# The second MLP product over both token halves at once, each of its seven products again split in seven

## The chip, the cores and the metric

The kernel runs on one core of one Trainium2 chip. TensorE (PE in the profile) multiplies matrices into PSUM; VectorE (DVE), ScalarE (ACT) and GpSimd (POOL) work element by element; SyncE (SP) issues the transfers between HBM and on-chip memory (SBUF). Each engine has its own instruction queue, works through it in order, and waits on semaphores of the others. The metric is the device time of one execution in microseconds; the time before is the median of three runs. All data are float32.

## The reference

A layer of an encoder with 2048 tokens of width 1024: a mixer with two groups of attention heads, an output projection, and an MLP of width 4096. Only the MLP matters for the change:

```python
h = rmsnorm(x, g_norm2[l]) * (1.0 + sc2) + sh2
x = x + gt2 * (jnp.square(jax.nn.relu(h @ w1[l])) @ w2[l])
```

`h` is 2048 x 1024, `w1` 1024 x 4096, `w2` 4096 x 1024. Below, `h @ w1` is the first product, the product with `w2` the second, and the squared ReLU between them gives the hidden values.

## The kernel before

**Precision.** TensorE multiplies in a rounded float32. To keep float32 accuracy, each operand is split in a high part (ACT copies it into the rounded type) and a low part (DVE subtracts the high part from the source): `split`, lines 123 to 125. A product of two tiles is then three matmuls, high x high, high x low and low x high (`mm3`). A split is thus one ACT and one DVE instruction for each tile of 128 x 512, and both inputs of the DVE instruction lie in SBUF.

**Seven products.** Both MLP products use a scheme in which a product of 2 x 2 blocks is formed from seven block products instead of eight (Winograd's form of Strassen's). The seven have numbers 1 to 7. Their operands are blocks or sums and differences of blocks, and the four result blocks are running sums of the products.

**Stages.** The tokens form two halves of 1024 (`mb` 1, then 0), each of two blocks of 512 (`TB`). For each half there are 7 x 16 steps of the first product (`First(mb, j, i)`; column group `j` of 16, product `i` of seven), then 7 x 16 steps of the second (`Second(mb, i, j)`). A step is 12 matmuls. `First` takes the activations from `hops[i, k]`, split tiles that stay in SBUF for a whole half, and splits its weight tile (`opw` in the profile). After each column group DVE and ACT form the hidden blocks (`hidden`: two ACT activations), and DVE the differences that the second product needs; SP stores all seven to HBM (`scr_hid`).

`Second` before: for product `i`, 16 row groups `j`, each step with a hidden tile and a weight tile of 128 x 512, both loaded from HBM in pairs (`hw`) and both split (`oph`, `opv`): two splits for 12 matmuls into four PSUM banks. At the end of each product four sums out of PSUM are made.

**Weight sums.** The first product's weight sums are four POOL sums in each column group (`sums`, tiles `ts` and `w`), with both inputs in SBUF. Those of `w2` are made while the first product of half 1 runs: `second_sums`, 64 DVE sums of 128 x 512 (`w2s`), stored to `scr_s`.

**Norm and blocks of half 0.** The norms of half 0 (`norm2`) and its activation blocks (`right_blocks(0, k, temp)`, scaled, split and subtracted on DVE and ACT) are spread over the second product of half 1.

**What sets the order.** The main loop at the end walks over the list `steps`. Before step `n` runs, it prepares (splits) the operands of later steps as long as at most 8 operand tiles are ready or in use (`opp`, 8 buffers). Then it runs the jobs that `at(n, job)` has entered for that step, then the step's matmuls and what follows them; `later.add(t, job)` runs a job t steps later. The order in which the program emits instructions is the order of each engine's queue. TensorE and SP keep exactly this order, and the other engines too work in the order of emission. Raw tiles come from `ring` (3 buffers) and `spare` (1), accumulators and kept blocks from `accp` (12), temporary ones from `tp` (7).

Of the kernel before, what the change touches and what calls it, by code (L numbers as in the profile page):

```python
# [18 lines left out]
P = 128  # L19
# [60 lines left out]
def encoder_kernel(ctx, tc, xT, c, g1, g2, w_in, w_rest, gqk, bias, w_o, w1, w2, w_ada, b_ada, out):  # L80
# [1202 lines left out]
    PRODUCTS = (1, 6, 5, 7, 2, 3, 4)  # L1283
    scr_hid = scratch("scr_hid", [P, 2, TB], 2, 8, NP // 2)
    scr_s = scratch("scr_s", [P, 2, TB], 7, NP // 2)

    pm = ctx.enter_context(ExitStack())
    if True:
# [42 lines left out]
        def norm2(tb, step):  # L1331
# [26 lines left out]
            for k in range(KT):  # L1358
                at(step + k, lambda k=k: load(k))
                at(step + k + 4, lambda k=k: add(k))  # L1360
            at(step + KT + 4, lambda: later.add(2, second))
# [54 lines left out]
        class Step:  # L1416
            tiles = frees = 1

            def prepare(self):
                pass  # L1420
# [4 lines left out]
        class First(Step):  # L1425
# [4 lines left out]
            def __init__(self, mb, j, i):  # L1430
                self.mb, self.j, self.i, self.nm = mb, j, i, f"{mb}_{j}_{i}"
                if mb and j == 0 and i in PRODUCTS[:2]:
                    self.tiles = self.frees = 0
# [35 lines left out]
            def run(self):  # L1469
                d, i, nm = First.pair[self.mb, self.j], self.i, self.nm  # L1470
                home = {2: 1, 4: 7}.get(i, i)
# [8 lines left out]
                if i == 1:  # L1480
                    d["u"] = kept(f"u{nm}")
                    act.copy(d["u"], ps)
                if i == 6:
                    column_sum(dve, d["u"], ps, d["u"], ALU.add)
                if i == 5:
                    d["v"] = column_sum(dve, kept(f"v{nm}"), ps, d["u"], ALU.add)
                if i == 7:
                    d["c22"] = self.hidden(column_sum(dve, kept(f"x{nm}"), ps, d["v"], ALU.add), 3)
# [6 lines left out]
                if i == 3:  # L1495
                    c12 = self.hidden(column_sum(dve, d["v"], ps, d["v"], ALU.add))

                    def rest():
                        t1 = column_sum(dve, kept(f"a{nm}"), c12, d["c11"], ALU.subtract)
                        self.keep(5, t1)  # L1500
                        d["t2"] = column_sum(dve, kept(f"b{nm}"), d["c22"], t1, ALU.subtract)
                        self.keep(6, d["t2"])
                        self.keep(7, column_sum(dve, c12, d["c22"], c12, ALU.subtract))

                    later.add(2, rest)
                if i == 4:
                    c21 = self.hidden(column_sum(dve, d["u"], ps, d["u"], ALU.add), 2)
# [17 lines left out]
        def second_sums(j, step):  # L1525
# [3 lines left out]
            def load():  # L1529
                t.append(raw_pair([P, 2, 2, TB], F32, f"w2s_{j}"))  # L1530
                for s in range(2):
                    sp.dma_start(t[0][:, s].rearrange("p r n -> p (r n)"), w2[2 * j + s])

            def out(i, dst, a, b, op):
                tile = {nm: t[0][:, s, r, :] for nm, s, r in (("11", 0, 0), ("21", 0, 1), ("12", 1, 0), ("22", 1, 1))}
                column_sum(dve, tile[dst], tile[a], tile[b], op)
                sp.dma_start(scr_s[i - 1 if i < 7 else 0, j // 2][:, j % 2, :], tile[dst])

            at(step - (6 if j else 0), load)
            sums = ((5, "22", "21", "22", ALU.add), (7, "21", "11", "21", ALU.subtract))  # L1540
            sums += ((6, "11", "22", "11", ALU.subtract), (3, "12", "12", "11", ALU.subtract))
            for n, x in enumerate(sums):
                at(step + n + (0 if j else 4), lambda x=x: out(*x))

        class Second(Step):


            tiles = frees = 2
            banks, raws, whole = {}, {}, {}

            def __init__(self, mb, i, j):
                self.mb, self.i, self.j, self.nm = mb, i, j, f"{mb}_{i}_{j}"

            def load(self):
                mb, i, j = self.mb, self.i, self.j
                t = raw_pair([P, 2, 2, TB], F32, f"hw{self.nm}")
                h, w = t[:, 0], t[:, 1]
                sp.dma_start(h, scr_hid[mb, i, j // 2])
                if i in (1, 2, 4):
                    r, s = {1: (0, 0), 2: (0, 1), 4: (1, 1)}[i]  # L1560
                    for q in range(2):
                        sp.dma_start(w[:, q, :], w2[2 * (j + q) + s][:, r * TB : (r + 1) * TB])
                else:
                    sp.dma_start(w, scr_s[i - 1 if i < 7 else 0, j // 2])
                Second.raws[mb, i, j // 2] = h, w

            def prepare(self):
                mb, i, j = self.mb, self.i, self.j
                h, w = Second.raws[mb, i, j // 2]
                self.h = operand(h[:, j % 2, :], f"h{self.nm}")  # L1570
                self.w = operand(w[:, j % 2, :], f"v{self.nm}")

            def run(self):
                mb, i, j = self.mb, self.i, self.j
                if j == 0:
                    Second.banks[i] = [bank(f"{self.nm}_{n}") for n in range(HK)]
                if i not in (1, 6, 5):
                    if j == NP // 2 - 1:
                        self.load_base()
                    if NP // 2 + 2 < j <= NP // 2 + 2 + HK:  # L1580
                        self.base(j - NP // 2 - 3)
                for n in range(HK):
                    ns = slice(n * P, (n + 1) * P)
                    mm3(
                        Second.banks[i][n], self.w[:, 0, ns], self.w[:, 1, ns], self.h[:, 0, :], self.h[:, 1, :],
                        j == 0, j == NP - 1,
                    )
                if j == NP - 1:
                    for n in range(HK):
                        self.out(n, Second.banks[i][n])  # L1590

            def load_base(self):
                i, d = self.i, Second.whole
                for n in range(HK):
                    d["x", n] = temp(f"x{self.nm}_{n}")
                    sp.dma_start(d["x", n], scr_x[2 * self.mb + (i in (2, 4)), n + HK * (i in (7, 4))])

            def base(self, n):

                i, d = self.i, Second.whole  # L1600
                nn = n + HK * (i in (7, 4))
                x, u = d["x", n], d[{7: "v", 2: "s", 3: "v", 4: "u"}[i], n]
                dve.scalar_tensor_tensor(x, u, mod[:, 5 * KT + nn : 5 * KT + nn + 1], x, op0=ALU.mult, op1=ALU.add)

            def out(self, n, ps):
                i, d = self.i, Second.whole
                tb = 2 * self.mb + (i in (2, 4))
                if i == 1:
                    d["s", n] = kept(f"s{self.nm}_{n}")
                    act.copy(d["s", n], ps)  # L1610
                    return
                if i == 6:
                    d["u", n] = column_sum(dve, kept(f"u{self.nm}_{n}"), ps, d["s", n], ALU.add)
                    return
                if i == 5:
                    d["v", n] = column_sum(dve, kept(f"v{self.nm}_{n}"), ps, d["u", n], ALU.add)
                    return
                if i == 7:
                    column_sum(dve, d["u", n], ps, d["u", n], ALU.add)
# [178 lines left out]
```

## Time and profile before

| | |
|---|---|
| median of three runs | 2596.46 us (2596.16 to 2598.76) |
| span of the profiled execution | 2595.2 us |
| stage of the first product, half 1 | 1365.7 to 1671.6 us |
| second product, half 1 | 1671.6 to 1977.5 us |
| first product, half 0 | 1977.5 to 2284.0 us |
| second product, half 0, and the end | 2284.0 to 2595.2 us |

In the profile, times are microseconds from the start of the span unless marked ns. A row of a group of instructions gives the engine, the operation, output <- inputs by the program's tile names, the shape, the count, then busy time in all and mean ns of one, then idle time just before and what ended it. A row of a tile gives minimum, median and maximum ns. A row of the view in order of time gives start, duration, engine and operation. Durations of neighbouring instructions of an engine can overlap by some 0.1 us, so the price of one in a dense row is taken from start to start. Every instruction of the kernel stands at line 42 (L42), since a helper there issues it; the tile names tell them apart.

### The profile page before, as it was taken

To read this page: it belongs to the slowest core of one execution; us is meant where nothing else is said; L and a number is where in the kernel's file an instruction comes from. 1 tells how busy PE (TensorE), PEld (TensorE's weight loads), DVE (VectorE), ACT (ScalarE), POOL (GpSimd) and SP (SyncE) were. 2 spreads that over 40 slices of the span, in tenths; PEclk is the share of its full clock that TensorE was granted. 3 is DMA by queue.
4 is the path that set the end of the run, shared out by engine and by line. 5 is a ranking of instruction groups with operands and counts; after the bars stand their busy time and mean duration, and the time that the engine had idled before them with its cause. 6 is when DMAs were issued, how large, how long until landed. Compare 5 with 4: busy or idle time off the path is not lost.

```text
span 2595.2 us, 39377 instructions
## 1 busy us (share of the span) xinstructions
PE 2571.3 (99%) x12628; PEld 2141.1 (83%) x12628; DVE 1886.0 (73%) x3233; ACT 1408.0 (54%) x2719; POOL 940.2 (36%) x1256
## 2 busy tenths in 40 slices
PE   9999999999999999999999999999999999999999
PEld 7888888888888888887888888888888888888887
DVE  7656767887799879998768777868766565655655
ACT  6333434668866686666744544556544544444443
POOL 4330154777766677776604333000002323200000
PEclk9999999999999999999999999999999999999999
DMA  9879879789887788756696777876764444375574
GB/s 350 333 295 364 329 293 280 222 246 273 267 257 242 237 276 249 256 172 208 207 363 244 264 266 249 308 263 240 253 228 172 142 153 156 128 267 196 193 272 154
DMA packets 251503, 640.20 MB, mean 247 GB/s; under 512 B 28576, under 2 KB 52128, under 8 KB 242208
## 3 DMA queue, kind: packets, MB, share of 16 engines
q1 hardware_dynamic: 250000, 632.96, 71.1%
q10 hardware_dynamic: 1296, 4.72, 0.4%
q8 instruction: 100, 1.64, 0.3%
q14 instruction: 107, 0.88, 0.1%
HBM read 446.20 MB, written 191.37 MB: 246 GB/s over the span
## 4 chain that ended last, share of the span: by engine, by line
PE 87%; DVE 5%; ACT 3%; issue 2%; DMA 2%; POOL 1%; SPq 1%; DVEq 0%; ACTq 0%; POOLq 0%
PE ps L42 45%; PE pt L42 11%; PE acc L42 6%; PE wt L42 6%; PE po L42 4%; PE z L42 4%; PE pf L42 4%; PE pq L42 3%; PE cz L42 2%; PE pso L42 2%; DVE p L42 2%; PE ct L42 1%; ACT z L42 1%; DVE wtl L42 1%; PE px L42 1%
## 5 line engine op out<-in xcount | busy, mean ns | idle before, releaser
L42 PE MATMUL ps<-oph,opv 128*128 128x512 f32 x2688 | 611.8, 389 | 0.2
L42 PE MATMUL ps<-h,opw 128*128 128x512 f32 x2664 | 605.2, 389 | 0.1
L42 PEld LDWEIGHTS ps<-oph,opv 128*128 128x128 f32 x2688 | 504.0, 188 | 106.1 <-DVE opv L42 0.8
L42 PEld LDWEIGHTS ps<-h,opw 128*128 128x128 f32 x2664 | 499.8, 188 | 105.2 <-DVE cx L42 0.9
L42 POOL TENSOR_TENSOR b<-p 128x512 f32<-128x512 f32 (+1 forms) x320 | 292.5, 914 | 167.9 <-DVE p L42 93.0
L42 ACT CAST wth<-wt 128x512 fp32r<-128x512 f32 (+3 forms) x544 | 257.4, 484 | 172.4 <-PE wt L42 162.4
L42 DVE TENSOR_TENSOR wtl<-wt,wth 128x512 fp32r<-128x512 f32 (+3 forms) x544 | 291.1, 547 | 59.3 <-ACT wth L42 56.8
L42 DVE TENSOR_TENSOR oph<-hw,oph 128x512 fp32r<-128x512 f32 x224 | 156.7, 700 | 214.4 <-ACT oph L42 214.3
L42 ACT CAST oph<-hw 128x512 fp32r<-128x512 f32 x224 | 139.3, 622 | 276.1 <-PE ps L42 266.0
L42 PE MATMUL pt<-w,ht 128*128 128x512 f32 x1248 | 288.2, 391 | 0.0
L42 POOL TENSOR_TENSOR ts<-w 128x512 f32<-128x512 f32 x32 | 44.0, 1375 | 666.3 <-DMA w<-in_w_dram 338.4
L42 PEld LDWEIGHTS pt<-w,ht 128*128 128x128 f32 x1248 | 233.0, 188 | 47.7
L42 DVE TENSOR_TENSOR_SCAN p<-z,p,zero 128x512 f32<-128x512 f32 x192 | 245.7, 1281 | 25.7 <-ACT z L42 18.8
L42 PE MATMUL acc<-wth,v 128*128 128x512 f32 (+3 forms) x544 | 220.6, 410 | 0.0
L42 ACT ACTIVATE z<-z 128x512 f32<-128x512 f32 (+1 forms) x320 | 166.5, 521 | 55.1 <-PE z L42 49.2
L42 PE MATMUL z<-k,q 128*128 128x512 f32 (+3 forms) x640 | 185.6, 371 | 7.6 <-DVE p L42 7.0
L42 PE MATMUL acc<-wtl,v 128*128 128x512 f32 (+3 forms) x544 | 185.4, 347 | 0.0
L42 DVE TENSOR_TENSOR opw<-w,opw 128x512 fp32r<-128x512 f32 x127 | 102.2, 807 | 113.2 <-ACT opw L42 113.1
L42 POOL TENSOR_TENSOR e<-e,cols 128x640 f32<-128x640 f32 (+4 forms) x128 | 143.0, 1123 | 83.2 <-DVE cols L42 57.0
L42 PE MATMUL wt<-ident,b 128*128 128x128 f32 x1088 | 171.4, 273 | 1.0 <-DVE cols L42 0.3
L42 PEld LDWEIGHTS wt<-ident,b 128*128 128x128 f32 x1088 | 136.4, 141 | 42.1 <-DVE cols L42 1.8
L42 PE MATMUL po<-fx,ow 128*128 128x512 f32 x576 | 161.6, 393 | 1.0 <-DMA ow<-scr_wo 1.0
(196 smaller groups left out, 4109.0 us busy)
## 6 DMA issues: line engine op xcount, KB each, us to landing
hw<-scr_hid SPq DMA_DIRECT2D x112, 512.0 KB, 3.8
q<-scr_q SPq DMA_DIRECT2D x128, 256.0 KB, 5.2
w<-in_w_dram SPq DMA_DIRECT2D x64, 512.0 KB, 5.3
hw<-scr_s SPq DMA_DIRECT2D x64, 512.0 KB, 4.6
k<-scr_k SPq DMA_DIRECT2D x240, 128.0 KB, 4.4
v<-scr_v SPq DMA_DIRECT2D x120, 256.0 KB, 4.0
wa<-in_w_ada_dram SPq DMA_DIRECT2D x48, 512.0 KB, 6.2
ow<-scr_wo SPq DMA_DIRECT2D x24, 1024.0 KB, 6.4
```

The costliest lines, as they stand in the source:

```text
L42: return lambda *x, **y: self.tc.keep_in_program_order(f(*x, **y))
```

## The change

The second product is made once, after both first products, over all 2048 tokens. Its outer seven products (`INNER`, index `a`, the numbers of the products whose hidden tiles `First` stored) are each a product of 2 x 2 blocks in themselves, and each is now formed from seven products again (`OUTER`, index `q`). So there are 7 x 7 x 8 steps with 6 matmuls each into two PSUM banks.

- A step splits one right tile of 128 x 512 (hidden values, `opr`), and every second step a left tile (two weight pieces of 128 x 256, `ol`).
- The hidden tiles are loaded as 128 x 1024 pieces (`half`, tile `b`), and POOL forms their differences in place (`half_sum`): 16 for each `a`.
- The sums of `w2` for the inner scheme stay on DVE; those for the outer one are new, on POOL (`outer_sums`): 32 sums of 128 x 4 x 256 in the first product of half 1 (`second_sums`) and 32 of 128 x 3 x 256 in that of half 0 (`third_sums`). They are stored to `scr_s` and `scr_t`.
- Results are gathered in twelve accumulators (`accs`, s, u, v by four blocks); sums with a product that was copied out of PSUM are made on POOL (`more`, and the v sums of product 5), sums out of PSUM on DVE (`result`), and the scaled sums into output rows on DVE (`add`).
- The first product runs its seven products in another order (`FIRST`), with one DVE sum out of PSUM fewer for each column group. It takes raw tiles from `ring` alone.
- The norms of half 0 move into the first product of half 1. The activation tiles of half 0 (`next_blocks`) are loaded and scaled within its last 13 steps, and `hops` is refilled one product after another over its last 7 steps.

```diff
-    PRODUCTS = (1, 6, 5, 7, 2, 3, 4)
+    FIRST = (1, 2, 5, 3, 6, 7, 4)
+    INNER = (1, 6, 2, 5, 7, 3, 4)
+    OUTER = (1, 5, 3, 6, 2, 7, 4)
+    HP = NP // 2
+    CN = TB // 2
     scr_hid = scratch("scr_hid", [P, 2, TB], 2, 8, NP // 2)
-    scr_s = scratch("scr_s", [P, 2, TB], 7, NP // 2)
+    SUMS = {6: 0, 7: 1, 3: 2, 5: 3}
+    BLOCKS = {1: 0, 2: 1, 4: 2}
+    scr_s = {pr: dram.tile([P, 4, HP, CN], F32, name=f"scr_s{pr}") for pr in range(1, 8)}
+    scr_t = {pr: dram.tile([P, 3, HP, CN], F32, name=f"scr_t{pr}") for pr in (3, 5, 6, 7)}
...
-                    t = raw_pair([P, 2, KT, P], F32, f"w1_{self.mb}_{j}")
+                    t = ring.tile([P, 2, KT, P], F32, tag="r8", name=f"w1_{self.mb}_{j}")
...
+                if i in (1, 5):
+                    d["p", i] = kept(f"p{nm}")
+                    act.copy(d["p", i], ps)
...
+                if i == 6:
+                    u = column_sum(dve, kept(f"u{nm}"), ps, d["p", 1], ALU.add)
+                    d["c12"] = self.hidden(column_sum(dve, u, d["ps", 5], u, ALU.add))
+                if i == 7:
+                    u = column_sum(dve, kept(f"v{nm}"), ps, d["p", 1], ALU.add)
+                    c22 = d["c22"] = self.hidden(column_sum(dve, d["p", 5], u, d["p", 5], ALU.add), 3)
...
+            def inner(n):
+                v = {nm: t[n][:, q].rearrange("p n c -> p (n c)") for q, nm in enumerate(("11", "21", "12", "22"))}
+                sums = (("22", "21", "22", ALU.add), ("21", "11", "21", ALU.subtract))
+                sums += (("11", "22", "11", ALU.subtract), ("12", "12", "11", ALU.subtract))
+                for dst, a, b, op in sums:
+                    column_sum(dve, v[dst], v[a], v[b], op)
+
+            def store(pr, n, h):
+                sp.dma_start(scr_s[pr][:, :, u, :], t[n][:, :, h, :])
+
+            at(step - 4, load)
+            for n in range(2):
+                at(step + n, lambda n=n: inner(n))
+            at(step + 1, lambda: store(1, 0, 0))
+            at(step + 2, lambda: [store(2, 1, 0), store(4, 1, 1)])
+            outer_sums(t, scr_s, slice(0, 4), u, step + 4)
...
+            def out(pr, dst, a, b, op):
+                v = {nm: t[n][:, cs, h, :] for nm, n, h in (("11", 0, 0), ("12", 1, 0), ("21", 0, 1), ("22", 1, 1))}
+                column_sum(pool, v[dst], v[a], v[b], op)
+                later.add(2, lambda: sp.dma_start(scr[pr][:, :, u, :], v[dst]))
...
+                if k % 2 == 0:
+                    m = k // 2
+                    o = Second.l = hop[m].tile([P, 2, 2, CN], F32R, tag=f"h3_{m}", name=f"ol{self.nm}")
+                    split(o[:, 0], o[:, 1], Second.raws[a, q][:, k : k + 2, :])
+                self.l = Second.l
+                nm = {1: "11", 5: "12", 3: "22", 6: "12", 2: "21", 7: "11", 4: "21"}[self.pr]
+                self.r = operand(Second.halves[a, nm, k // 2][:, k % 2, :], f"r{self.nm}")
 
             def run(self):
+                pr, k = self.pr, self.k
+                home = HOME[pr]
+                for n in range(2):
+                    if k == 0 and home == pr:
+                        Second.banks[home, n] = bank(f"{self.nm}_{n}")
+                    ps = Second.banks[home, n]
                     ns = slice(n * P, (n + 1) * P)
                     mm3(
+                        ps, self.l[:, 0, k % 2, ns], self.l[:, 1, k % 2, ns], self.r[:, 0, :], self.r[:, 1, :],
+                        k == 0 and home == pr, k == HP - 1, home != pr,
                     )
+                if k == HP - 1:
+                    self.end()
...
+            def more(self, blocks):
+
+                for b, pr in blocks:
+                    begun = (b, self.a) in Second.outs
+                    if self.i in (1, 5) and not begun:
+                        Second.outs[b, self.a] = [Second.outs["p", pr][:, n, :] for n in range(2)]
+                        continue
+                    before = Second.outs[b, self.a] if begun else accs["s" if self.i == 6 else "", b] if self.i == 6 else self.target(b)
+                    for n in range(2):
+                        column_sum(pool, self.target(b)[n], before[n], Second.outs["p", pr][:, n, :], ALU.add)
+                    Second.outs[b, self.a] = self.target(b)
+
+            def result(self, b, *banks):
+
+                i, t = self.i, self.target(b)
+                before = Second.outs.pop((b, self.a), None)
+                if before is None and i not in (1, 5):
+                    before = accs["s", b] if i == 6 else t
+                if i in OUTS and i != 7:
+                    self.add(b, before)
+                    for ps in banks:
+                        self.add(b, ps)
+                    self.give(b)
                     return
+                for ps in banks:
+                    for n in range(2):
+                        if before is None:
+                            act.copy(t[n], ps[n])
+                        else:
+                            column_sum(dve, t[n], ps[n], before[n], ALU.add)
+                    before = t
                 if i == 5:
+                    for n in range(2):
+                        column_sum(pool, accs["v", b][n], accs["u", b][n], t[n], ALU.add)
...
+        def half_sum(a, dst, x, y, g):
+            h = Second.halves
+            column_sum(pool, h[a, dst, g], h[a, x, g], h[a, y, g], ALU.subtract)
...
+        def second(begin):
+
+            steps.extend(Second(begin, a, q, k) for a in range(7) for q in range(7) for k in range(HP))
+            for a in range(7):
+                f = begin + 7 * HP * a
+
+                for g in range(HP // 2):
+                    at(f - 18 + 2 * g if a else begin - 6 + g // 2, lambda a=a, g=g: half(a, "11", g, "h1"))
+                    at(f - 14 + 2 * g if a else begin - 5 + g // 2, lambda a=a, g=g: half(a, "12", g, "h2"))
+                    at(f - 4 + 2 * g if a else begin - 3 + g // 2, lambda a=a, g=g: half(a, "22", g, "h5"))
+                    at(f + 13 + 2 * g, lambda a=a, g=g: half(a, "21", g, "h5"))
+                    at(f - 5 + 2 * g if a else begin - 2 + g // 2, lambda a=a, g=g: half_sum(a, "12", "12", "11", g))
+                    at(f + 11 + 2 * g, lambda a=a, g=g: half_sum(a, "12", "22", "12", g))
+                    at(f + 27 + 2 * g, lambda a=a, g=g: half_sum(a, "11", "12", "11", g))
+                    at(f + 35 + 2 * g, lambda a=a, g=g: half_sum(a, "21", "21", "12", g))
+                for q in range(7):
+                    s = steps[f + HP * q]
+                    at(f + HP * q - 18 if a or q > 2 else begin - 4 + q, s.load)
...
+            def fill(i, nm):
                 for k in range(HK):
+                    hops[i, k] = hop[k].tile([P, 2, TB], F32R, tag=f"h{i}_{k}", name=f"h0_{i}_{k}")
+                    split(hops[i, k][:, 0, :], hops[i, k][:, 1, :], y[k, nm])
+
+            def less(eng, nm, a, b):
+                for k in range(HK):
+                    column_sum(eng, y[k, nm], y[k, a], y[k, b], ALU.subtract)
...
+            for k, n in enumerate((-13, -13, -14, -13)):
+                at(end + n, lambda k=k: load(k))
+                at(end + n + 4, lambda k=k: scale(k))
+            fills = ((1, "11"), (2, "21"), (5, "11"), (3, "22"), (6, "22"), (7, "12"), (4, "21"))
+            after = {1: (pool, "11", "12", "11"), 5: (pool, "12", "22", "12"), 3: (dve, "22", "22", "11")}
+            after |= {6: (pool, "21", "21", "22")}
...
-            if mb:
-                end = len(steps)
-                norm2(1, end - 8)
-                norm2(0, end)
...
+                norm2(1, begin + 18)
+                norm2(0, begin + 48)
+        second(len(steps))
...
-            while nxt is not None and ready - used + nxt.tiles <= 8:
+            while nxt is not None and ready - used + nxt.tiles <= 8 and n >= nxt.earliest:
```

More of the change, by code (lines that the diff above doesn't have):

```diff
@@ L1527, in second_sums, with third_sums @@
+        def third_sums(u, step):
             t = []
             def load():
[L1530 to L1537, printed above, removed]
@@ L1542, in second_sums @@
             for n, x in enumerate(sums):
-                at(step + n + (0 if j else 4), lambda x=x: out(*x))
+                at(step + n // 2, lambda x=x: out(*x))
         class Second(Step):
[L1548 to L1552, printed above, removed]
-            def load(self):
[L1555 to L1562, printed above, removed]
-                else:
-                    sp.dma_start(w, scr_s[i - 1 if i < 7 else 0, j // 2])
-                Second.raws[mb, i, j // 2] = h, w
@@ L1567, in prepare @@
-            def prepare(self):
[L1568 to L1571, printed above, removed]
-            def run(self):
[L1574 to L1582, printed above, removed]
+            loads, raws, halves, outs, banks = {}, {}, {}, {}, {}
@@ L1588, in run @@
[L1588 to L1603, printed above, removed]
```

186 lines of the change are left out of this document (136 added, 50 removed).

## Prediction, made before the changed kernel ran

> **What bounds the kernel now.** I read the page first, for the span, the busy shares and the granted clock, then the busy times by stage, then DVE and POOL in order of time inside the first MLP product.
>
> ```profile
> span 2595.2 us, 39377 instructions
> PE 2571.3 (99%) x12628; PEld 2141.1 (83%) x12628; DVE 1886.0 (73%) x3233; ACT 1408.0 (54%) x2719; POOL 940.2 (36%) x1256
> PEclk9999999999999999999999999999999999999999
> L42 PE MATMUL ps<-oph,opv 128*128 128x512 f32 x2688 | 611.8, 389 | 0.2
> ```
>
> TensorE (PE) is busy for 99% of the span at an undisturbed clock, and the second MLP product alone is 2688 matmuls and 611.8 us. The 389 ns of one are pipelined, so the price of a matmul has to come from a stage. The stages are, in order: all that lies before the MLP, first product of half 1, second product of half 1, first of half 0, second of half 0 with the end.
>
> ```profile
> core 0: us, PE busy (x) PEld busy (x) DVE busy (x) ACT busy (x) POOL busy (x), PEclk, DMA share, GB/s
> 0.00:1365.70 1365.70, 1346.48 (x7220) 1129.02 (x7221) 1065.77 (x2041) 822.29 (x1693) 746.93 (x1121) 1.00 0.81 272
> 1365.70:1671.60 305.90, 305.84 (x1346) 252.00 (x1345) 243.63 (x321) 146.55 (x260) 97.15 (x62) 1.00 0.74 262
> 1671.60:1977.50 305.90, 305.74 (x1362) 252.43 (x1361) 218.86 (x347) 162.65 (x288) 11.28 (x15) 1.00 0.69 248
> 1977.50:2284.00 306.50, 306.50 (x1354) 253.88 (x1353) 183.79 (x257) 147.15 (x253) 84.82 (x59) 1.00 0.43 153
> 2284.00:2595.20 311.20, 306.76 (x1354) 253.76 (x1352) 173.91 (x270) 129.35 (x228) 0.00 (x0) 1.00 0.60 211
> ```
>
> Each MLP stage is 1344 matmuls, and 305.9/1344 = 0.2276 us is what one costs. The last stage holds 305.9 us of them and an end of 5.3 us. The second column to look at is DVE: 243.6 of 305.9 us in the first product of half 1, with POOL beside it at 97 us, but only 219 and 174 us in the two second products, where POOL hardly runs (11 us and none). What DVE and POOL do to each other is seen in the first product, DVE's rows ahead and POOL's behind:
>
> ```profile
> start us, us, engine line op out<-in xcount [idle before <-releaser]
> 1480.90 1.78 DVE L42 TENSOR_TENSOR w2s<-w2s 128x512 f32<-128x512 f32 x1
> 1482.60 0.68 DVE L42 TENSOR_TENSOR cv<-ps,cv 128x512 f32<-128x512 f32 x1
> 1485.15 0.69 DVE L42 TENSOR_TENSOR opw<-w,opw 128x512 fp32r<-128x512 f32 x1 [1.87 <-ACT opw L42]
> ...
> 1489.53 0.68 DVE L42 TENSOR_TENSOR opw<-ts,opw 128x512 fp32r<-128x512 f32 x1
> 1490.13 0.68 DVE L42 TENSOR_TENSOR cu<-ps,cu 128x512 f32<-128x512 f32 x1
> 1490.73 0.68 DVE L42 TENSOR_TENSOR opw<-ts,opw 128x512 fp32r<-128x512 f32 x1
> ...
> 1497.47 1.77 DVE L42 TENSOR_TENSOR w2s<-w2s 128x512 f32<-128x512 f32 x1
> 1499.17 1.77 DVE L42 TENSOR_TENSOR opw<-ts,opw 128x512 fp32r<-128x512 f32 x1
> 1500.87 1.77 DVE L42 TENSOR_TENSOR w2s<-w2s 128x512 f32<-128x512 f32 x1
> 1502.57 0.68 DVE L42 TENSOR_TENSOR cv<-ps,cv 128x512 f32<-128x512 f32 x1
> ...
> 1482.09 1.74 POOL L42 TENSOR_TENSOR w<-w 128x512 f32<-128x512 f32 x1
> ...
> 1497.08 1.62 POOL L42 TENSOR_TENSOR ts<-ts,w 128x512 f32<-128x512 f32 x1
> 1498.66 1.74 POOL L42 TENSOR_TENSOR w<-w 128x512 f32<-128x512 f32 x1
> 1500.36 1.73 POOL L42 TENSOR_TENSOR ts<-w,ts 128x512 f32<-128x512 f32 x1
> ```
>
> Alone, DVE starts an operation of 512 columns every 0.60 us (1489.53, 1490.13, 1490.73). Against POOL it starts one every 1.70 us (1497.47, 1499.17, 1500.87), and POOL one every 1.58 to 1.70: they take turns, one operation each. This holds for DVE operations with both inputs in SBUF; the sum with an input in PSUM at 1482.60 took its usual 0.68 us in the middle of POOL's operation at 1482.09. So a POOL sum of 512 columns costs a pressing DVE 1.70 - 0.60 = 1.10 us. Before, this shows on the chain of waits only in spots of a few us:
>
> ```profile
> 1612.75 1.79 DVE w2s L42
> 1614.54 1.69 DVE opw L42
> 1616.23 1.70 DVE w2s L42
> ```
>
> **The change, part by part.**
>
> *Matmuls.* In the built order the second product has 7 x 7 x 8 steps of 6 matmuls, 2352 in place of 2688; no other count changes. 336 x 0.2276 = 76.5 us less on TensorE. If TensorE stayed the bound, the span would be 2518.7 us.
>
> *Splits.* Every step splits its right tile in two parts (ACT the high, DVE the low), and every second step a left tile: 1.5 splits for 6 matmuls (1.37 us), before 2 for 12 (2.73 us). That is 84 splits in each of the seven inner products, 588 in all, before 448. All have both inputs in SBUF. ACT needs 1.5 x 0.62 = 0.93 us of 1.37, so it keeps up; its price is in the row of its cast below. DVE alone would need 0.90 us.
>
> *Sums on POOL.* New in the second product are 112 differences of tiles of 1024 columns (16 for each inner product) and 52 sums of 512 columns that start or finish accumulators. The price of a POOL sum:
>
> ```profile
> L42 ACT CAST oph<-hw 128x512 fp32r<-128x512 f32 x224 | 139.3, 622 | 276.1 <-PE ps L42 266.0 <-DMA hw<-scr_hid 10.1
> L42 POOL TENSOR_TENSOR ts<-w x32: 1285/1298/1790, 1362.5 to 2239.5; 128x512 f32<-128x512 f32 x32
> L42 POOL TENSOR_TENSOR b<-p 128x512 f32<-128x512 f32 x224 | 233.5, 1042 | 155.2 <-DVE p L42 89.5 <-PE wt L42 19.2 <-PE z L42 16.3
> L42 POOL TENSOR_TENSOR b<-p 128x256 f32<-128x256 f32 x32 | 19.7, 615 | 3.3 <-DVE p L42 0.5 <-PE wt L42 0.5 <-PE po L42 0.2
> ```
>
> A sum of two tiles takes 1.29 us undisturbed. The b rows give the fixed part: 1042 - 615 = 427 ns for 256 columns, so 615 - 427 = 188 ns fixed. 1.29 - 0.19 = 1.10 us is just what DVE lost above, so I take it that DVE is shut out for the variable part. No sum of 1024 columns is in this trace. With the ts rows it shuts DVE out for 2 x 1.10 = 2.20 us, with the b rows' 1.67 ns a column for 1.71 us, and if its fixed part counts too for 2 x 1.30 = 2.60; below all, it costs nothing where DVE happens to be idle. I take 2.20, since ts like the new sums reads two different tiles.
>
> The Trainium skill (GPSIMD Engine Reference, Elementwise — side-by-side cycle accounting) has 4497 ns measured for a two-input sum of 2048 columns. Half of it, 2.25 us less the fixed 0.19, is an estimate of 2.06 us per sum of 1024; the forecast would be 144 x 0.14 = 20 us lower by it.
>
> *The sum for the second product.* DVE with two SBUF inputs: 588 splits and 40 scaled sums into output rows, 628 x 0.60 = 377 us. DVE sums out of PSUM: 66 x 0.60 = 40 us, of which I take half to run while POOL has its turn, 20 us. POOL's turns: 112 x 2.20 + 52 x 1.10 = 246 + 57 = 303 us. Together 700 us against 535 us of matmuls. This assumes that DVE hardly idles. The operand pool holds 8 tiles, 7 steps ahead of the matmul. After each inner product's first stretch its six accumulator sums and eight tile differences stand back to back on POOL, some 36 us in which DVE gets about 20 splits through, 13 steps; the 7 steps are used up, TensorE waits, and DVE then never gets far enough ahead to idle. So DVE and POOL, taking turns, set the pace: 700 + 5 us of end, where 617.1 us stood (305.9 + 311.2).
>
> *First product, half 1.* DVE was busy 243.6 us here. By the two orders it gets 51 more operations with two SBUF inputs (the norms of half 0 and the scaling of its 16 blocks, formerly under the second product, among them), +31, and 15 fewer out of PSUM, -9. The outer weight sums go to POOL, 32 sums of 1024 columns: 32 x 2.20 = +70. That makes 336 us against 305.8 us of matmuls. DVE also idles 1.87 us (row 1485.15) where a split waits for ACT behind the two activations of a hidden block; two such places in each of 16 column groups, 60 us, were covered by the slack before. POOL's turns can fall into them now. I take 10 us uncovered: 346 us, between 306 (all of POOL's new turns in idle time) and 396.
>
> *First product, half 0.* DVE 183.8 us; +52 x 0.60 = 31, -13 x 0.60 = -8, 12 more POOL sums of 512 at 1.10 = 13, and 32 of 768 columns at 1.65 = 53: 273 us, up to 333 with the uncovered idle time, against 306.5. At its start, though, the 28 splits that refill the activations, formerly spread over the second product, come within 7 steps (19 us) beside that stage's own work. They need 17 us of DVE alone. I take +6: 312 us, between 306 and 333.
>
> *Edits costed at nothing:* the new order of the seven first products (same matmuls, a sum fewer out of PSUM), the other weight layout and the transfers:
>
> ```profile
> hw<-scr_hid SPq DMA_DIRECT2D x112, 512.0 KB, 3.8
> hw<-scr_s SPq DMA_DIRECT2D x64, 512.0 KB, 4.6
> hw<-in_w_dram SPq DMA_DIRECT2D x96, 256.0 KB, 5.4
> ```
>
> The hidden and weight tiles of the second product come to 112 x 0.5 + 49 x 1 MB = 105 MB on the SP queue, before 56 + 32 + 24 = 112 MB, and DMA shares of 0.43 to 0.74 leave room; loads are issued 10 steps ahead of their splits. If that cover is gone, the late thing is a left tile, some 5 us for each of 49.
>
> *Sum.* 1365.7 + 346 + 312 + 700 + 5 = 2729 us of span; the median of the runs stands 1.3 us above the span (2596.46 to 2595.2), so **2730 us**.
>
> **The rivals.**
>
> *TensorE stays the bound (faster).* It is one mechanism: a POOL sum of 1024 columns costs DVE little, since it falls where DVE would wait for TensorE, or lets several DVE operations pass. If it cost p, the second product would be 454 + 112p and the first product of half 1 276 + 32p, at least 306. With the 6 us of the other half this equals the time before at 454 + 112p + 32p - 30 + 6 = 617 - 5, p = 1.26 us, and below (535 - 454)/112 = 0.72 us TensorE alone decides. Then 2519 to 2545 us. For it speaks that DVE idles 62 us in the first product of half 1 and 87 and 137 us in the second ones; against it, that at 1.37 us a step DVE has just 0.47 us to spare, and that turns of 1.10 us show wherever both press.
>
> *The block is cheaper.* With the b rows' 1.71 us: 144 x 0.49 = 71 us less, and with the idle places filled 10 more, about 2650 us, down to 2600.
>
> *DVE and POOL wait for each other as well.* In the first product the sums that a split needs stand on POOL behind four weight sums, 4 x (2.20 + 0.60) = 11 us, and a ring slot is only loaded anew once POOL's last sum is stored. Where the 7 steps of lead are spent, DVE idles in addition: some 5 us in each of 16 weight groups, and 21 us more in half 0: 2830 us.
>
> The Trainium skill (SBUF — State Buffer, Who interferes with whom) says that whichever of the two starts first holds the shared port pair for its whole instruction. By that rule the block grows with the columns, as in the forecast; the rows here show it for 512 columns alone.
>
> **How the numbers follow.** Forecast, 2660 to 2790: 0.56. Cheaper block, 2600 to 2660: 0.10. Waits on top, 2790 and more: 0.15, of which 0.01 over 2850. Faster: 0.17. About the same: 0.02. The range 2600 to 2850 leaves out the faster case, the equal one and that end. Its lower end is the cheaper price with the first products near their lower bounds; its upper end is the idle time uncovered. Taking 0.2% as what a measurement can tell from no change: faster 0.17, same 0.02, slower 0.81.
>
> **What would show it.** Right: in the second product the splits on DVE (opr, ol) have a mean well over 1 us with many near 2.8, POOL's sums of 1024 columns 2.4 to 2.9 us, TensorE about 76% busy there (535 of 700), and DVE heads the chain of waits. The stage then takes about 700 us and the first product of half 1 about 345. Wrong, if the splits stay at 0.7 us and TensorE at 99%; if POOL's sums of 1024 take under 1.5 us; or if the time lies in waits for DMA, ACT or the ring's slots.

## The result and the profile after

The changed kernel takes 2984.64 us (median of four runs, 2982.56 to 2987.31) against 2596.31 us in the same series: 1.1495 times the time, 95% interval 1.1479 to 1.1512. It is slower, as forecast, but by 388 us in place of 134, and outside the range. Three rows of the page of the changed kernel's profile.

```profile
span 2981.4 us, 39238 instructions
PE 2631.2 (88%) x12292; PEld 2121.5 (71%) x12292; DVE 2293.1 (77%) x3379; ACT 1512.5 (51%) x2915; POOL 1558.0 (52%) x1496
PEclk9999999999999999999998997999999999998999
```

The two kinds of MLP matmul in its groups by shape (count, then busy time and mean ns of one, then TensorE's idle time just before them and the three releasers that ended most of it):

```profile
L42 PE MATMUL ps<-h,opw 128*128 128x512 f32 x2664 | 684.7, 414 | 191.7 <-ACT cp L42 76.6 <-DVE cv L42 63.4 <-DVE cu L42 51.7
L42 PE MATMUL ps<-opr,ol 128*128 128x512 f32 x2352 | 589.3, 411 | 130.8 <-DVE opr L42 73.4 <-DVE tx L42 25.1 <-ACT p L42 12.0
```

The two MLP stages as windows of the same trace: both first products, then the second product with the end.

```profile
core 0: us, PE busy (x) PEld busy (x) DVE busy (x) ACT busy (x) POOL busy (x), PEclk, DMA share, GB/s
1364.40:2256.60 892.20, 695.49 (x2721) 529.67 (x2720) 554.72 (x651) 352.03 (x610) 369.92 (x217) 0.93 0.57 202
2256.60:2981.40 724.80, 589.55 (x2353) 462.48 (x2352) 673.90 (x688) 336.62 (x611) 441.12 (x160) 0.92 0.45 164
```

The second product takes 724.8 us; 705 were forecast. The first products take 892.2 us, where 346 + 312 = 658 were forecast and 612.4 stood before. So nearly all of the miss, 234 of 255 us, lies in the first products, whose matmuls did not change at all. Counting 1344 matmuls on, half 1 takes 484 us and half 0 409. What TensorE waited for there is in the first matmul row: copies (cp) that ACT makes out of PSUM, and sums (cv, cu) that DVE makes out of PSUM. DVE itself is busy for only 555 of 892 us. The timeline of TensorE over one column group of half 0:

```profile
start us, us, engine line op out<-in xcount [idle before <-releaser]
2094.99 5.73 PE L42 MATMUL ps<-h,opw 128*128 128x512 f32 x24 [0.83 <-DVE cv L42]
2101.40 5.74 PE L42 MATMUL ps<-h,opw 128*128 128x512 f32 x24 [0.68 <-ACT cp L42]
2107.82 5.74 PE L42 MATMUL ps<-h,opw 128*128 128x512 f32 x24 [0.68 <-ACT cp L42]
2114.34 3.06 PE L42 MATMUL ps<-h,opw 128*128 128x512 f32 x12 [0.78 <-DVE cu L42]
```

TensorE stops four times in a group, always between two products that accumulate in the same bank (`HOME`): 1 and 2, 5 and 3, 6 and 7, 7 and 4. In the new order they are neighbours. Product 2 must not add to the bank until ACT has copied product 1 out of it, and no other matmul stands between them. Even where ACT does this at once, 0.68 us pass.

In the second product the forecast's picture is there. From the timeline of the changed kernel, DVE's rows and then POOL's (start, us, and the count of operations that a row sums up):

```profile
2379.94 2.90 DVE L42 TENSOR_TENSOR ol<-l,ol 128x512 fp32r<-128x512 f32 x1
2382.76 4.55 DVE L42 TENSOR_TENSOR opr<-b,opr 128x512 fp32r<-128x512 f32 x2
...
2376.63 8.43 POOL L42 TENSOR_TENSOR b<-b,b 128x1024 f32<-128x1024 f32 x3
```

The same POOL sums in the view of their tile (shortest, median and longest ns of one, and from when to when):

```profile
L42 POOL TENSOR_TENSOR b<-b,b x112: 2345/2825/8809, 2235.3 to 2943.5; 128x1024 f32<-128x1024 f32 x112
```

And DVE's splits in the groups by shape:

```profile
L42 DVE TENSOR_TENSOR opr<-b,opr 128x512 fp32r<-128x512 f32 x392 | 413.8, 1088 | 7.7 <-ACT opr L42 7.6
```

A split that meets a POOL sum of 1024 columns starts 2.82 us before the next (2379.94 to 2382.76), and the three sums take 8.43 us, 2.81 each: turns of one operation each. An undisturbed split starts 0.60 us before the next, so DVE is shut out for about 2.2 us. Undisturbed, the POOL sum takes 2.35 us.

### The profile page after: what moved, and what is told of

Read it like the earlier page. It is cut to its first block, busy times and chain, and to the rows that moved or that the text cites. A ratio compares the mean times of both kernels' runs of the same rounds, so it can differ in the third digit from the quotient of the medians.

```text
span 2981.4 us, 39238 instructions
## 1 busy us (share of the span) xinstructions
PE 2631.2 (88%) x12292; PEld 2121.5 (71%) x12292; DVE 2293.1 (77%) x3379; ACT 1512.5 (51%) x2915; POOL 1558.0 (52%) x1496
## 4 chain that ended last, share of the span: by engine, by line
PE 54%; DVE 24%; issue 7%; ACT 7%; DMA 4%; POOL 2%; SPq 0%; DVEq 0%; ACTq 0%; POOLq 0%
PE ps L42 19%; PE pt L42 9%; DVE opr L42 8%; PE acc L42 5%; PE wt L42 5%; DVE ol L42 4%; PE z L42 4%; PE pf L42 3%; PE po L42 3%; PE pq L42 2%; ACT cp L42 2%; DVE tx L42 2%; PE cz L42 1%; DVE cu L42 1%; DVE p L42 1%
## 5 line engine op out<-in xcount | busy, mean ns | idle before, releaser
L42 PE MATMUL ps<-h,opw 128*128 128x512 f32 x2664 | 684.7, 414 | 191.7 <-ACT cp L42 76.6
L42 PE MATMUL ps<-opr,ol 128*128 128x512 f32 x2352 | 589.3, 411 | 130.8 <-DVE opr L42 73.4
L42 PEld LDWEIGHTS ps<-opr,ol 128*128 128x128 f32 x2352 | 462.7, 199 | 257.5 <-DVE opr L42 97.1
L42 POOL TENSOR_TENSOR b<-b,b 128x1024 f32<-128x1024 f32 x112 | 354.1, 3184 | 199.0 <-DMA b<-scr_hid 93.1
L42 DVE TENSOR_TENSOR opr<-b,opr 128x512 fp32r<-128x512 f32 x392 | 413.8, 1088 | 7.7 <-ACT opr L42 7.6
L42 ACT CAST ol<-l 128x512 fp32r<-128x512 f32 x196 | 121.9, 622 | 354.5 <-PE ps L42 351.1
L42 ACT CAST opr<-b 128x512 fp32r<-128x512 f32 x392 | 224.7, 616 | 12.5 <-POOL b L42 12.5
L42 DVE TENSOR_TENSOR ol<-l,ol 128x512 fp32r<-128x512 f32 x196 | 202.1, 1031 | 36.1 <-ACT ol L42 35.9
L42 DVE TENSOR_TENSOR opw<-w,opw 128x512 fp32r<-128x512 f32 x126 | 124.2, 987 | 110.9 <-ACT opw L42 109.0
L42 DVE TENSOR_TENSOR opw<-ts,opw 128x512 fp32r<-128x512 f32 x96 | 86.7, 910 | 151.0 <-ACT opw L42 150.8
```

Source lines behind the costliest of these rows:

```text
L42: return lambda *x, **y: self.tc.keep_in_program_order(f(*x, **y))
```

## The experiments

Theory: two causes. In the first products neighbours share a PSUM bank; in the second DVE and POOL take turns. Rivals: the first products are held up by POOL's new sums, the norms and the refill; the second by waits for its banks. Each kernel was run once, beside a run of the kernel before (2594.9 to 2596.9 us); the four runs of the changed kernel lie within 5 us, so differences of a few us are not read. Times of the stages run from the first matmul of a stage to that of the next; only the row of the kernel before takes the borders given above (from first matmul to first matmul it has 610 and 619). The runs that leave work out (x4, x5, x6, x8) only show what that work costs.

| run | total | first products | second |
|---|---|---|---|
| before | 2596 | 612 | 617 |
| changed | 2985 | 892 | 725 |
| x2: before, new order | 2760 | 773 | 619 |
| x9: before, order spread | 2718 | 733 | 619 |
| x12: before, spread, own bank for 4 | 2630 | 644 | 619 |
| x1: changed, old order and banks | 2874 | 768 | 739 |
| x5: x1, no outer weight sums | 2799 | 692 | 739 |
| x6: x1, no refill | 2829 | 725 | 738 |
| x8: x1, no refill, no norms | 2808 | 705 | 739 |
| x3: changed, differences on DVE | 2904 | 890 | 648 |
| x4: changed, no differences | 2860 | 898 | 593 |
| x7: x1, all new sums on DVE | 2739 | 733 | 641 |
| x10: changed, spread | 2908 | 812 | 728 |
| x13: changed, spread, own bank | 2893 | 793 | 733 |
| x11: x10, all new sums on DVE | 2839 | 838 | 633 |
| x14: x13, all new sums on DVE | 2806 | 797 | 643 |

**The order alone (x2), put in the kernel before.**

```diff
-            steps += [First(mb, j, i) for j in range(NP) for i in PRODUCTS]
+            steps += [First(mb, j, i) for j in range(NP) for i in FIRST]
-                home = {2: 1, 4: 7}.get(i, i)
+                home = HOME[i]
...
```

> The kernel before with only the new order of the first product, its shared banks and its sums. Theory (bank chain): at least 0.68 + 0.68 + 0.78 + 0.83 = 3 us of waits in each of 32 column groups, 96 us, and more where ACT or DVE stand behind other work: 2690 to 2760 us. Rival (the order costs nothing by itself, POOL's new sums and the refill do): 2585 to 2605 us.

2760.5 us, 165 more, all of it in the first products (399 and 374 us): the rival that the order costs nothing falls. The waits are those of the changed kernel, here in x2's timeline of TensorE:

```profile
1499.63 5.74 PE L42 MATMUL ps<-h,opw 128*128 128x512 f32 x24 [0.68 <-ACT cp L42]
1506.04 5.74 PE L42 MATMUL ps<-h,opw 128*128 128x512 f32 x24 [0.68 <-ACT cp L42]
1513.41 3.01 PE L42 MATMUL ps<-h,opw 128*128 128x512 f32 x12 [1.63 <-DVE cu L42]
1517.91 5.74 PE L42 MATMUL ps<-h,opw 128*128 128x512 f32 x24 [1.48 <-DVE cv L42]
```

**Neighbours, or shared banks as such (x9, x12).** Banks and sums of the new order are kept, only the products are put apart; x12 then gives product 4 a bank of its own.

```diff
-    FIRST = (1, 2, 5, 3, 6, 7, 4)
+    FIRST = (1, 5, 2, 6, 3, 7, 4)
+    BANK = {**HOME, 4: 4}
-                home = HOME[i]
+                home = BANK[i]
```

> The kernel before with the new order's banks and sums, but the products in the order 1, 5, 2, 6, 3, 7, 4: of the products that share a bank only 7 and 4 are still neighbours, the others are one or two products apart. Theory (a neighbour in the same bank waits until ACT or DVE has read it): only the wait ahead of product 4 is left, 0.8 to 1.5 us in each of 32 groups, the time is 2620 to 2660 us, against 2760 with the new order. Rival (the new sums or the shared banks cost the time, not the neighbours): 2730 us or more.

> The kernel before with the order 1, 5, 2, 6, 3, 7, 4 and a bank of its own for product 4, so that no neighbours share a bank (1 and 2, 5 and 3, 6 and 7 still do, one or two products apart). In the run with 7 and 4 as neighbours (2718 us) all waits for DVE's or ACT's reading stood ahead of product 4, 2.4 us each. Theory (neighbours): they go, 2596 to 2630 us. Rival (shared banks or the new sums as such cost the time): 2680 us or more.

x9 took 2718.2 us, a miss for the theory and short of the rival's 2730: the one pair left cost 121 us, more than the 96 that were read off the four. What TensorE waits for before its matmuls into PSUM, by releaser (us in all, then the count of waits), in x9:

```profile
  DVE cv L42: 76.0, 32
  ACT cp L42: 2.8, 1
  DVE cu L42: 1.7, 5
```

The same view of x12:

```profile
  ACT cp L42: 26.2, 21
  DVE cu L42: 0.6, 1
```

The waits between the three separated pairs are gone (2.8 and 1.7 us), and all of it stands at the pair 7 and 4, 2.4 us a group. There DVE's read (cv) has other work ahead of it in its queue. From x9's timeline, DVE's rows, and below them the matmuls that wait:

```profile
1508.23 0.68 DVE L42 TENSOR_TENSOR cu<-ps,cu 128x512 f32<-128x512 f32 x1
1510.78 0.69 DVE L42 TENSOR_TENSOR opw<-w,opw 128x512 fp32r<-128x512 f32 x1 [1.86 <-ACT opw L42]
1511.38 0.68 DVE L42 TENSOR_TENSOR w2s<-w2s 128x512 f32<-128x512 f32 x1
1511.98 0.68 DVE L42 TENSOR_TENSOR cv<-ps,cp 128x512 f32<-128x512 f32 x1
...
1512.72 19.16 PE L42 MATMUL ps<-h,opw 128*128 128x512 f32 x72 [4.11 <-DVE cv L42]
```

The split ahead waits 1.86 us for ACT, which has the two activations of a hidden block in front of its cast. So the price of a neighbour is not the read alone but all that the reading engine has queued before it. With a bank for product 4 (x12) the time is 2629.7 us: 131 of the 165 us are gone once no neighbours share a bank. The other 34 us remain, 26 of them where ACT's copy of product 1 is late even with one product between.

**The old order in the changed kernel (x1).**

```diff
-    FIRST = (1, 2, 5, 3, 6, 7, 4)
+    FIRST = (1, 6, 5, 7, 2, 3, 4)
-                home = HOME[i]
+                home = {2: 1, 4: 7}.get(i, i)
...
```

> The changed kernel with the first product's old order (1, 6, 5, 7, 2, 3, 4), its old banks and its old sums; the refill of the activations follows that order. Theory (bank chain): in the new order products 1 and 2, 5 and 3, 6 and 7, 7 and 4 are neighbours and share a PSUM bank, so TensorE waits for ACT or DVE to read the bank, and that is the time above the forecast in the first products. Then they fall from 433 and 460 us to the forecast's 346 and 312 or so, and the time from 2985 to 2720 to 2790 us. Rival (the new POOL sums and the refill hold up DVE there): the first products stay near 430 and 460 us, the time above 2930.

2873.9 us: theory and rival both lost, each in part. (The 433 and 460 us named there were split at 1797 us, too early; by the count of matmuls the halves of the changed kernel took 484 and 409.) The first products fall by 124 us, but to 768 us, not to 658. The two stages of x1 as windows, columns as above, and then its first products by halves:

```profile
1365.90:2133.70 767.80, 651.57 (x2721) 528.19 (x2719) 578.36 (x639) 324.85 (x570) 377.02 (x217) 0.92 0.65 230
2133.70:2872.20 738.50, 597.25 (x2352) 467.98 (x2352) 691.59 (x700) 341.97 (x622) 445.93 (x160) 0.91 0.45 166
...
1365.90:1791.00 425.10, 338.83 (x1376) 272.44 (x1375) 331.49 (x366) 170.83 (x299) 210.22 (x121) 0.90 0.67 237
1791.00:2133.70 342.70, 312.73 (x1346) 255.74 (x1344) 246.87 (x274) 154.01 (x272) 166.81 (x97) 0.96 0.63 220
```

In half 1 DVE is busy for 331 us, where the prediction had added up 336. But the stage lasts 425 us, so DVE stands idle for 94 us of it; the prediction took 10. The largest part of its idle time is that before the splits of weights, which wait for ACT (over both halves, groups by shape of x1):

```profile
L42 DVE TENSOR_TENSOR opw<-w,opw 128x512 fp32r<-128x512 f32 x127 | 133.8, 1055 | 111.0 <-ACT opw L42 111.0
```

**What holds the first products then (x5, x6, x8).** From x1, POOL's outer weight sums left out; the refill left out; the refill and the norms left out.

```diff
-                column_sum(pool, v[dst], v[a], v[b], op)
...
-        next_blocks(KT + 7 * NP)
...
-                norm2(1, begin + 18)
-                norm2(0, begin + 48)
```

> The changed kernel with the first product's old order and banks (2874 us), and the 64 outer weight sums on POOL left out (their tiles are stored unsummed). With the old order the first products still take some 424 and 344 us, where 346 and 312 were forecast. Theory (turns): the outer sums shut DVE out for 70 and 53 us; without them the first product of half 1 falls by 50 to 70 us, that of half 0 by 5 to 30, the time to 2770 to 2820 us. Rival (norms and refill, which were moved there, take the time): 2850 us or more.

> The same kernel (old order, 2874 us) without the refill: the activations of half 0 are not loaded, scaled and split, and the first product of half 0 runs on those of half 1. Theory (the refill comes in one lump that DVE and ACT cannot hide): some 45 to 60 us of waits round the border of the two first products go, the time is 2810 to 2835 us. Rival (its 17 to 30 us of DVE work is hidden in the lead of 7 steps): 2860 us or more.

> As the run without the refill, and without the norms of half 0 too (their loads, squares, sums and the two turns through POOL and TensorE). Theory: TensorE waits for the norm's row, which stands behind POOL's weight sums, and DVE has 14 sums fewer: 15 to 30 us less than without the refill alone. Rival (the norms are hidden): within 5 us of it.

All three came as the theory had it: 2799.3, 2829.2 and 2807.8 us. In the first products the outer sums are worth 768 - 692 = 76 us, the refill 43 and the norms 20, together 139 of the 156 us by which x1 stands above the kernel before, if they add up; no run leaves out all three. So the rival of the first theory is no rival but a second cause of similar size. Its way to TensorE is the same, a bank read too late. The first products' matmuls in the groups by shape, of x1 and then of x5:

```profile
L42 PE MATMUL ps<-h,opw 128*128 128x512 f32 x2664 | 642.3, 404 | 97.7 <-DVE cx L42 69.9 <-ACT cu L42 15.4 <-ACT h L42 8.1
L42 PE MATMUL ps<-h,opw 128*128 128x512 f32 x2664 | 623.5, 396 | 50.9 <-DVE cx L42 24.6 <-ACT cu L42 14.0 <-ACT h L42 8.1
```

DVE's cx reads product 7 out of the bank in which product 4 goes on, with two products between them. In the kernel before these matmuls wait 0.1 us in all, in x1 69.9 us for cx alone. Without the outer sums DVE is busy 102 us less over the first products (476 us against 578), and the wait falls to 24.6 us.

**The second product (x3, x4).** The differences of hidden tiles on DVE, or left out.

```diff
-            column_sum(pool, h[a, dst, g], h[a, x, g], h[a, y, g], ALU.subtract)
+            column_sum(dve, h[a, dst, g], h[a, x, g], h[a, y, g], ALU.subtract)
```

> The changed kernel with the 112 differences of 1024 columns on DVE in place of POOL, all else as it was. Theory (DVE and POOL take turns in the second product): each costs DVE about 1.13 us of its own in place of 2.20 us shut out; DVE then has 377 + 127 + 57 + 20 to 40 = 580 to 600 us of work, the second product falls from 725 to 590 to 620 us, the time to 2850 to 2880. Rival (the second product waits for its banks to be read, and DVE is the one that reads them): more work on DVE makes it no shorter, 2985 us or more.

> The changed kernel with the 112 differences of hidden tiles left out, so that the second product multiplies the undiminished tiles. Theory (turns): DVE has 377 + 57 + 20 = 454 us of work, less than the 535 us of matmuls; the second product falls from 725 to 540 to 580 us, the time to 2800 to 2840. Rival (waits for banks): above 2940 us.

More work on DVE made it faster: 2904.3 us, the second product 648 us in place of 725. Left out, 2859.8 us and 593. Both stay above the expectation by 13 to 28 us, but the rival (no gain) falls. Groups by shape of x3:

```profile
L42 PE MATMUL ps<-opr,ol 128*128 128x512 f32 x2352 | 561.5, 400 | 81.6 <-DVE tx L42 23.6 <-DVE opr L42 19.9 <-DVE u L42 14.1
L42 DVE TENSOR_TENSOR opr<-b,opr 128x512 fp32r<-128x512 f32 x392 | 286.2, 746 | 1.7 <-ACT opr L42 1.7
L42 DVE TENSOR_TENSOR b<-b,b 128x1024 f32<-128x1024 f32 x112 | 140.6, 1256 | 0.0
```

The split's mean falls from 1088 to 746 ns, and a difference costs DVE 1.26 us itself, less than the 2.2 us for which POOL's shut it out. Of the 113 us left above 535, some 62 us are waits for sums and copies out of PSUM (tx, u, cs, p), 20 us waits for splits, and 26 us longer matmuls (561.5 us for 535 us of work, at a granted clock of 0.94). Whether other banks would help here was not tried.

**Both undone (x7, x10, x11, x13, x14).** x7 is x1 with the sums that the change gave to POOL on DVE, all but twelve small ones of the refill; x10 and x13 are the spread order in the changed kernel, without and with the bank for product 4; x11 and x14 the same with the sums on DVE.

> The changed kernel with the old order and banks, and with every sum that the change put on POOL on DVE: the 112 differences, the 64 outer weight sums and the 52 accumulator sums. Theory (turns): each costs DVE its own 1.13, 0.87 or 0.60 us in place of 2.20, 1.65 or 1.10 us shut out; the second product falls from 734 to 590 to 630 us, the first products by 30 to 60 us together, the time to 2700 to 2750 us. Rival (DVE's own work is the bound wherever it comes from): 2800 us or more.

> The changed kernel with the first product in the order 1, 5, 2, 6, 3, 7, 4, banks kept, the second weighted sum of product 5 and 3 made after 3, the refill in that order. Theory (neighbours in a bank): nearly as much is gained as by the old order and old banks (2874 us), with 0.8 to 1.5 us in 32 groups lost: 2870 to 2920 us. Rival (the old sums made the difference there): 2950 us or more.

> The changed kernel with this order and this bank. Theory: better than the old order with the old banks (2874 us), since fewer banks wait: 2800 to 2880 us; what then is left above the forecast is POOL's turns, the refill and the norms. Rival: as without the bank, about 2908 us.

> The same with all sums that the change put on POOL on DVE. Both causes then are weakened, by another way than in the run with the old order (2739 us): 2730 to 2790 us if the two add up, above 2850 us if the order's gain was bound up with the old banks.

> The same with all sums that the change put on POOL on DVE. Theory: both causes undone, 2660 to 2740 us, at or below the run with the old order (2739 us); still slower than before, for the second product alone takes 628 to 641 us there against 617. Rival (order and turns are bound up): above 2800 us.

x7 came as expected, 2739.0 us (its second product, 641 us, a little above the range), the fastest of the changed forms that leave nothing out, and still 143 us above the kernel before. x10 did too (2907.9), but x13 (2893.1) and x11 (2839.5) lie between theory and rival, and in x14 (2806.3) the rival came: order and turns are bound up. In x14 TensorE still waits for ACT's copy of product 1, in the view by releaser:

```profile
  ACT cp L42: 111.4, 24
  DVE tx L42: 24.5, 3
```

One of these waits in x14's timeline, ACT's rows, and below them the matmuls that wait:

```profile
1453.38 1.29 ACT L42 ACTIVATE cp<-cp 128x512 f32<-128x512 f32 x2 [4.14 <-DVE cp L42]
1454.57 0.60 ACT L42 CAST opw<-w 128x512 fp32r<-128x512 f32 x1
1455.08 0.58 ACT L42 COPY cp<-ps 128x512 f32<-128x512 f32 x1
...
1455.71 22.09 PE L42 MATMUL ps<-h,opw 128*128 128x512 f32 x84 [8.78 <-ACT cp L42]
```

ACT is not busy, it stands 4.14 us waiting: the copy has the hidden block of product 4 ahead of it in ACT's queue, and that waits for DVE. One product between two users of a bank was nearly enough in the kernel before (26 us), but not here, where DVE is later; the old order has three between 1 and 2.

The sums on DVE help the second product each time (739 to 641, 728 to 633, 733 to 643 us). The first products they help in the old order alone (768 to 733 us); in the spread order these take 838 us in place of 812, where TensorE's wait for DVE's cv rises from 105 to 141 us, and with the bank for product 4 they stay (797 and 793 us). No form tried beats the kernel before.

## Why the prediction was wrong

- *The step that failed:* "Edits costed at nothing: the new order of the seven first products (same matmuls, a sum fewer out of PSUM)". The order was costed by counts of instructions; that it made neighbours of products with one bank, and so put four reads by ACT and DVE on TensorE's path in each of 32 groups, was not looked at. It is worth 165 us in the kernel before and 111 us in the changed one. Under the old order other products stood between the two users of a bank and hid those reads; the prediction did not ask what hid them.
- *A term mis-sized:* with the old order (x1) the time is still 2874 us, above the range, and the first products take 156 us more than before where 46 were forecast. POOL's outer sums, norms and refill measured 76, 20 and 43 us. DVE's load in half 1 was right (336 us forecast, 331 measured), but of DVE's idle time 10 us were taken as uncovered, and 94 us were. The refill's 6 us were too few; that its 28 splits and 16 scalings find DVE late already, so that the lead of 7 steps is used up, is argued and not shown.
- *Second product:* right. 705 us forecast, 725 measured; POOL's sum of 1024 columns 2.4 to 2.9 us forecast, 2.35 the shortest and 2.83 the median; DVE shut out 2.20 us, some 2.2 measured, so the block does grow with the columns (1.10 us at 512); the splits' mean well over 1 us forecast, 1.09 measured; TensorE 76% forecast, 81% measured at a granted clock of 0.92. The cheaper block is refuted, and so is the rival in which TensorE stays the bound. The estimate from the figure of the Trainium skill (GPSIMD Engine Reference, Elementwise — side-by-side cycle accounting), 2.06 us, was the further one.
- *Matmuls:* 336 fewer, as forecast. But the price of 0.2276 us did not hold: with TensorE waiting, each new start cost some 0.28 us more and the granted clock fell to 0.93 and 0.92 (last section).
- *Waits on top,* as a rival, named the ring's slots and POOL's queue; the waits that came were at PSUM banks.

## What to carry to other kernels

When a change reorders accumulations, write down the PSUM bank beside each one and count the matmuls between one user's end and the next user's start; that distance must cover the read and all that stands in the reader's queue ahead of it, and the distance needed grows when that engine, or one that its queue waits for, gets more work. Before giving sums to POOL to relieve DVE, compare what the sum costs DVE itself with what it shuts DVE out for: here 1.26 against 2.2 us. But a sum moved to DVE also stands in DVE's queue, ahead of reads that TensorE may wait for: in the spread order the first products gained nothing by the move. A scheme that saves matmuls pays in element-wise work, and that has to be priced on the engine that will then be the last.

## What was not expected of the hardware

TensorE ran its matmuls at half speed after longer waits. From its timeline in the changed kernel:

```profile
1423.55 7.37 PE L42 MATMUL ps<-h,opw 128*128 128x512 f32 x24 [2.14 <-ACT cp L42]
1832.23 5.49 PE L42 MATMUL ps<-h,opw 128*128 128x512 f32 x12 [11.87 <-DVE cu L42]
```

Twelve matmuls take 5.49 us after a wait of 11.87 us (granted clock 0.50 from 1832.3 to 1837.7 us), and 3.06 us after one of 0.78 (the row at 2114.34; granted clock 1.00 there). The Trainium skill (TensorE: Matmul & The Clock Gate, Part 1: The HAM clock gate) says that the clock falls to half after an idle window of about 3.4 us. The trace agrees in the factor, but shows slow matmuls behind shorter waits too: 24 matmuls take 7.37 us after 2.14 us, in place of 5.74. Of the ten waits between 2.0 and 2.5 us in this MLP eight were followed by slow matmuls (over 0.35 us from start to start), of the 112 between 0.6 and 1.5 us none.

Not all of the longer busy time is the clock. Each new start costs some 0.28 us besides its wait: 24 matmuls after one of 0.68 us take 5.74 us, and 24 x 0.2276 = 5.46. The kernel before and x2, whose granted clock was 0.99 and 1.00 in its two first products, show it in the groups by shape:

```profile
L42 PE MATMUL ps<-h,opw 128*128 128x512 f32 x2664 | 605.2, 389 | 0.1
L42 PE MATMUL ps<-h,opw 128*128 128x512 f32 x2664 | 644.1, 396 | 115.4 <-ACT cp L42 44.6 <-DVE cv L42 38.3 <-DVE cu L42 32.5
```

Some 130 starts make 39 us. In the changed kernel TensorE is busy 695 us over the first products for 612 us of matmuls at full speed, and 590 us over the second for 535: 137 us more. Some 130 and 55 starts at 0.28 us are about 51 us of this. The rest, some 85 us by this estimate, between a fifth and a quarter of the whole loss, is the lower clock, on top of the waits themselves.
